# An encoder trunk on one core: every engine in program order, with wider feed-forward products

## The chip, the cores and the metric

The kernel runs on one core of a Trainium2 chip. The core has a matrix engine (TensorE, PE in the profile), a vector engine (VectorE, DVE), a scalar engine (ScalarE, ACT), a general engine (GpSimd, POOL) and a queue that starts transfers (SyncE, SP). PE writes its products to PSUM, which has eight banks of 128 partitions by 512 fp32 numbers here; everything else lives in SBUF. Each engine works through its own queue in order, and the queues meet only at semaphores. The metric is the device time of one execution in microseconds; a lower time is better.

## The reference

Two layers (`DEPTH`) of an encoder work on 256 tokens of 1024 channels. Cut to what matters:

```python
proj = x @ w_in[i]                                   # 13,824 columns, split into ten parts
y_a = multiscale_pool(a_in) @ w_branch_a[i]
y_b = dilated_attention_mixer(q, k, v) @ w_branch_b[i]
y_c = hgrn2_bidirectional(q_h, i_h, ff_h, fb_h, g_h) @ w_branch_c[i]
merged = sigmoid(gate0) * y_a + sigmoid(gate1) * y_b + sigmoid(gate2) * y_c
x1 = layer_norm(ALPHA * x + merged @ w_out[i], ln1_g[i], ln1_b[i])
hidden = silu(x1 @ w_ffn_gate[i]) * (x1 @ w_ffn_up[i])
ple = (p[i] @ w_ple_proj[i]) * sigmoid(x1 @ w_ple_gate[i])
x = layer_norm(ALPHA * x1 + hidden @ w_ffn_down[i] + ple, ln2_g[i], ln2_b[i])
```

The recurrence (`hgrn2_bidirectional`) runs in both directions over eight heads; within blocks it is written as products of scaled queries and keys. All is fp32.

## The kernel before

**Weights.** All weights are read once, as 107 chunks a layer of 1 MB, in the order of use. A chunk is loaded by SP (`dma_chunk`, L190) into one of three `raw` buffers and split by `split_chunk` (L201): ACT writes the rounded high part `whi` (L210), DVE the rest `wlo` (L211), three buffers each. `use_chunk` hands the pair to PE. A product of two split operands is three products on PE: high by high, high by low, low by high (`mm3`, L250). The residual stream is kept split as well (`xh`, `xl`), transposed to channels by tokens.

**Forms of products.** `gemm_cols` (L256) holds 128 weight columns in the array and streams 256 tokens past them, so 48 products of 256 columns use one chunk. `tok_block` (L284) holds 128 tokens and streams 512 weight columns; it takes both chunks of a block for token tile 0 and then for tile 1, and calls its evacuation after each tile. `rows_gemm` (L806) does the two row-wise projections, `w_out` (4 chunks) and `w_ffn_down` (11 chunks), into four banks: the last 2 or 3 chunks are held back, run for tile 0, then for tile 1, and each tile's layer norm (L317) follows its sums.

**Steps and background.** After each chunk `step_end` (L245) splits a later chunk and calls `background` (L225), which gives 3,000 units to the first three tasks of a list. A task is a generator; it yields its estimated cost after each piece, or `None` to sleep until the next step. Tasks are the recurrence of two heads (`hgrn_task`, L348: on DVE scans, reciprocals and scalings for each direction; then PE products L431 within blocks, L439 and L444 across blocks; masks, products L468/L469 with the values, a root mean square by four squares on ACT and a power on POOL (L302), scalings L484, a transpose and a split), attention of one head (`attn_task`, L501: scores, softmax on DVE and ACT, transposes, products L536 to L539, for two token tiles), pooling, and a transposition of the merged branches (`turn`). One recurrence task may hold the work buffers at a time (`busy`). `finish(kind)` (L241) drains tasks at once where their results or buffers are needed; `finish("attn0")` stands at L701, after the product of chunk 4 of the second pair of heads.

**Order.** The planner of the tile framework orders each engine's queue from the dependences, the order of writing and its own cost model. Only the very start is pinned: L592 to L652 put ACT, DVE and PE in program order for the first block. Elsewhere the planner may move an instruction ahead of others on its engine, transfers included: the table `p` is loaded through ACT's queue at L796, right ahead of its transposes (L802), after which `ln1`'s gains are loaded and `rows_gemm` runs. The PSUM banks are two pools of four, `g` for chunk products and `t` for the tasks.

**Feed-forward.** For each of 11 pairs of chunks, gate and up go into one bank each; ACT takes the silu (L873), DVE the product with up (L876), and `split_to` (L290) splits the result.

## Time and profile before

| | before |
|---|---|
| median of 3 runs | 1334.33 us (1334.32 to 1334.39) |
| profiled execution, its own time | 1334.35 us |
| span from first to last instruction | 1332.6 us |
| mean granted clock of TensorE | 0.996 |
| DMA, mean over the span | 175 GB/s, 51.6% of the 16 engines on SP's queue |

How to read the profile: PE and PEld are TensorE's products and its weight loads. A number like L211 is a line of the kernel; where a helper records every operation, all have one line, and the names of the tiles tell them apart (`wlo<-raw,whi` is written from `raw` and `whi`). In the timeline the columns are start and duration in microseconds, engine, line, operation, tiles, shape, count, and in brackets the idle time ahead with what ended it. Products are pipelined, so the duration of one is longer than the distance to the next. In groups, the last numbers are busy microseconds, mean nanoseconds of one, and idle time just before.

### The profile page before, as it was taken

How to read it: one execution, taken by the hardware profiler on the slowest of the kernel's cores; microseconds unless marked ns; L12 is line 12 of the kernel's file. 1: busy time of each engine (PE TensorE's matmuls, PEld its weight loads, DVE VectorE, ACT ScalarE, POOL GpSimd, SP SyncE). 2: the span in 40 equal slices, each digit the busy share in tenths (PEclk: the TensorE clock that was granted, in tenths of full speed). 3: DMA queues.
4: the chain of work that ended last, by engine and by line, in shares of the span. 5: the costliest groups of instructions: out<-in, count | busy, mean ns of one | idle time of the engine just before them, and what ended most of it. 6: DMA issues, size and time to landing. Idle time of an engine off the chain costs nothing.

```text
span 1332.6 us, 20047 instructions
## 1 busy us (share of the span) xinstructions
PE 1308.5 (98%) x8585; PEld 1185.8 (89%) x8585; DVE 867.5 (65%) x1126; ACT 587.1 (44%) x644; POOL 16.7 (1%) x24
## 2 busy tenths in 40 slices
PE   8999999999999999999989999999999999999997
PEld 6899999998888799998779999999988887999986
DVE  4598887575656855554555999875846658554445
ACT  5444444544444443443334444445534444444431
POOL 0000000000000000000000000000000000000000
PEclk9999999999999999999989999999999999999999
DMA  8654545244556475655356555442455664755551
GB/s 310 196 185 158 166 151 159 96 158 159 197 190 228 151 233 179 189 190 190 126 176 203 169 172 166 158 159 90 134 189 190 202 217 154 226 189 190 180 194 38
DMA packets 160280, 233.43 MB, mean 175 GB/s; under 512 B 3840, under 2 KB 108864, under 8 KB 160192
## 3 DMA queue, kind: packets, MB, share of 16 engines
q1 hardware_dynamic: 158496, 227.44, 51.6%
q10 hardware_dynamic: 1696, 4.72, 1.1%
q8 instruction: 67, 1.10, 0.3%
q14 instruction: 21, 0.17, 0.0%
HBM read 231.10 MB, written 1.05 MB: 174 GB/s over the span
## 4 chain that ended last, share of the span: by engine, by line
PE 93%; DVE 4%; ACT 1%; issue 1%; POOL 1%; DMA 0%; POOLq 0%; DVEq 0%; ACTq 0%
PE g L252 28%; PE g L253 28%; PE g L254 28%; DVE wlo L211 2%; PE t L444 1%; PE t L431 1%; PE t L439 1%; PE t L312 1%; POOL rs_y L302 1%; PE t L468 1%; PE t L469 1%; ACT whi L210 0%; DVE ln_st L326 0%; PE t L508 0%; PE t L528 0%
## 5 line engine op out<-in xcount | busy, mean ns | idle before, releaser
L211 DVE TENSOR_TENSOR wlo<-raw,whi 128x2048 fp32r<-128x2048 f32 (+2 forms) x218 | 489.8, 2249 | 347.4 <-ACT whi L210 347.0
L210 ACT ACTIVATE whi<-raw 128x2048 fp32r<-128x2048 f32 (+2 forms) x218 | 409.9, 1883 | 517.5 <-issue 220.7
L252 PE MATMUL g<-xh,whi 128*128 128x256 f32 x1600 | 455.6, 285 | 0.0
L254 PE MATMUL g<-xh,wlo 128*128 128x256 f32 x1600 | 453.1, 283 | 0.0
L253 PE MATMUL g<-xl,whi 128*128 128x256 f32 x1600 | 453.0, 283 | 0.0
L252 PEld LDWEIGHTS g<-xh,whi 128*128 128x128 f32 x1600 | 307.0, 192 | 0.2
L253 PEld LDWEIGHTS g<-xl,whi 128*128 128x128 f32 x1600 | 307.0, 192 | 0.2
L254 PEld LDWEIGHTS g<-xh,wlo 128*128 128x128 f32 x1600 | 306.9, 192 | 0.0
L252 PE MATMUL g<-whi,xh 128*128 128x512 f32 x480 | 190.2, 397 | 1.3 <-ACT whi L210 1.2
L253 PE MATMUL g<-wlo,xh 128*128 128x512 f32 x480 | 189.5, 395 | 1.4 <-DVE wlo L211 1.4
L254 PE MATMUL g<-whi,xl 128*128 128x512 f32 x480 | 188.1, 393 | 0.0
L253 PEld LDWEIGHTS g<-wlo,xh 128*128 128x128 f32 x480 | 91.8, 191 | 21.4 <-DVE wlo L211 3.1
L252 PEld LDWEIGHTS g<-whi,xh 128*128 128x128 f32 x480 | 91.8, 191 | 21.2 <-ACT whi L210 1.8
L254 PEld LDWEIGHTS g<-whi,xl 128*128 128x128 f32 x480 | 91.6, 191 | 19.1
L253 PE MATMUL g<-wlo,s 128*128 128x512 f32 x224 | 87.5, 391 | 0.0
L254 PE MATMUL g<-whi,s 128*128 128x512 f32 x224 | 87.5, 390 | 0.0
L252 PE MATMUL g<-whi,s 128*128 128x512 f32 x224 | 87.1, 390 | 0.0
L252 PE MATMUL g<-whi,sa 128*128 128x512 f32 x160 | 62.8, 393 | 0.0
L253 PE MATMUL g<-wlo,sa 128*128 128x512 f32 x160 | 62.5, 390 | 0.0
L254 PE MATMUL g<-whi,sb 128*128 128x512 f32 x160 | 62.3, 389 | 0.0
L253 PEld LDWEIGHTS g<-wlo,s 128*128 128x128 f32 x224 | 42.1, 188 | 9.0 <-DVE wlo L211 0.4
L254 PEld LDWEIGHTS g<-whi,s 128*128 128x128 f32 x224 | 42.0, 188 | 8.6
(168 smaller groups left out, 1136.2 us busy)
## 6 DMA issues: line engine op xcount, KB each, us to landing
raw<-in_w_in_dram SPq DMA_DIRECT2D x106, 1024.0 KB, 5.1
raw<-in_w_ffn_gate_dram SPq DMA_DIRECT2D x22, 1024.0 KB, 5.3
raw<-in_w_ffn_up_dram SPq DMA_DIRECT2D x22, 1024.0 KB, 5.3
raw<-in_w_ffn_down_dram SPq DMA_DIRECT2D x22, 1024.0 KB, 4.9
raw<-in_w_branch_c_dram SPq DMA_DIRECT2D x8, 1024.0 KB, 5.1
raw<-in_w_branch_a_dram SPq DMA_DIRECT2D x8, 1024.0 KB, 5.0
raw<-in_w_out_dram SPq DMA_DIRECT2D x8, 1024.0 KB, 4.9
raw<-in_w_ple_gate_dram SPq DMA_DIRECT2D x8, 1024.0 KB, 5.1
```

What stands on the lines that cost most here:

```text
L210: A.activation(out=hi[:, ks, :], in_=t[:, ks, :], func=AF.Copy)
L211: V.tensor_tensor(out=lo[:, ks, :], in0=t[:, ks, :], in1=f(hi[:, ks, :]), op=ALU.subtract)
L252: PE.matmul(ps, lhsT=ah, rhs=bh, start=first, stop=False)
L253: PE.matmul(ps, lhsT=ah, rhs=bl, start=False, stop=False)
L254: PE.matmul(ps, lhsT=al, rhs=bh, start=False, stop=last)
L302: G.tensor_tensor(out=y, in0=v, in1=mhalf.to_broadcast([P, n]) if n > 1 else mhalf, op=ALU.pow)
L312: PE.transpose(ps[:, k * P:(k + 1) * P], xt[:, t, (4 * hf + k) * P:(4 * hf + k + 1) * P], ident)
L431: PE.matmul(dg[po:po + 64, co:co + 64], lhsT=KI[:, cs], rhs=QI[:, cs], start=True, stop=True)
L439: PE.matmul(cr[po:po + 64, co:co + 64], lhsT=KL[:, h, 4 * t, :], rhs=QL[:, h, 4 * t, :], start=True, stop=True)
L444: PE.matmul(lg[:, co:co + P], lhsT=kp.rearrange("p b u -> p (b u)"), rhs=qp.rearrange("p b u -> p (b u)"), start=True, stop=True)
L468: PE.matmul(o, lhsT=at[:, 2 * h + t, :], rhs=vt[:, t, hs], start=True, stop=False)
L469: PE.matmul(o, lhsT=al[:, 2 * h + 1 - t, :], rhs=vt[:, 1 - t, hs], start=False, stop=True)
```

## The change

Four engines (ACT, DVE, PE and POOL) issue in program order for the whole kernel; SP is left to the planner. The order is written anew. `step_end` runs background work first, then an evacuation that is handed to it, then the split. `tok_block` uses chunk by chunk for both token tiles. The norms become a class whose sums are added early; between stages, `Handover` puts tile 0's norm under tile 1's last products, and tile 1's norm under the first products of the next stage; two chunks' splits go in quarters there, their low parts on POOL.

Three products change. The feed-forward products take the high weights against 512 columns, the high and low parts of the tokens side by side in `xx`, and the low weights against 256; the halves are added afterwards. In the recurrence, direction 0 keeps its scaled blocks, and both directions' cross-block products run together after direction 1, those that write the two halves of the partitions in turn. And the order of the three products of a token block may be by pass, so that the low parts come last.

```diff
+    ctx.enter_context(tc.manual_schedule(engines={
+        mybir.EngineType.Activation, mybir.EngineType.DVE, mybir.EngineType.PE, mybir.EngineType.Pool}))
...
-    def split_chunk():
+    def split_begin():
...
+        def piece(ks, engine=V):
+            A.activation(out=hi[:, ks, :], in_=t[:, ks, :], func=AF.Copy)
+            engine.tensor_tensor(out=lo[:, ks, :], in0=t[:, ks, :], in1=f(hi[:, ks, :]), op=ALU.subtract)
+            if ks.stop == k:
+                dma_chunk()
+        return k, piece
...
-    def step_end():
+    def step_end(then=None):
+        background()
+        if then is not None:
+            then()
         split_chunk()
-        background()
...
+    def gemm_wide(w, ps):
+        for m in range(2):
+            ms = slice(m * P, (m + 1) * P)
+            for k in range(KD):
+                wide = (ps[m], w[0][:, k, ms], xx[:, k].rearrange("p a t -> p (a t)"))
+                narrow = (ps[m][:, 0:S], w[1][:, k, ms], xx[:, k, 0, :])
+                for i, (o, a, b) in enumerate((wide, narrow) if k == 0 else (narrow, wide)):
+                    PE.matmul(o, lhsT=a, rhs=b, start=k == 0 and i == 0, stop=k == KD - 1 and i == 1,
+                              skip_group_check=True)
+
+    def joined(ps, dst):
+        for m in range(2):
+            A.activation(out=dst[:, m, :], in_=ps[m][:, 0:S], func=AF.Copy)
+            V.tensor_tensor(out=dst[:, m, :], in0=dst[:, m, :], in1=ps[m][:, S:2 * S], op=ALU.add)
...
+    def tok_block(act, evac, n=2):
+        ps = [gbank(), gbank()]
+        for i in range(n):
+            w = use_chunk()
+            for t in range(2):
+                tok_part(ps[t], w, i, n, act, t)
+            step_end((lambda: [evac(t, ps[t]) for t in range(2)]) if i == n - 1 else None)
...
+        def rest(self, then=None):
...
+            G.tensor_tensor(out=y, in0=ve, in1=mhalf, op=ALU.pow)
+            cs = [slice(512 * hf, 512 * hf + 512) for hf in range(2)]
+            for c in cs:
+                V.scalar_tensor_tensor(out=xt[:, t, c], in0=xt[:, t, c], scalar=mv[:, 0:1], in1=gb[:, 0, c],
+                                       op0=ALU.subtract, op1=ALU.mult)
+            r = small([P, 1], "ln_r")
+            newton(r, y, ve, 1)
...
             u = 31 if fwd else 0
-            tot = c4(Ct)[:, :, :, :, u:u + 1]
+            tot = small([P, 2, 4, 2, 1], "tot")
+            V.tensor_copy(out=tot, in_=c4(Ct)[:, :, :, :, u:u + 1])
...
+            across.append((QL, KL))
             if d == 0:
-                cr, lg = tbank(), tbank()
+                continue
+            cr, lg = tbank(), tbank()
             for h in range(2):
                 for t in range(2):
-                    po = 0 if fwd else 64
                     co = (2 * h + t) * 64
-                    PE.matmul(cr[po:po + 64, co:co + 64], lhsT=KL[:, h, 4 * t, :], rhs=QL[:, h, 4 * t, :],
-                              start=True, stop=True)
...
+                    for po, (Q, K) in zip((0, 64), across):
+                        PE.matmul(cr[po:po + 64, co:co + 64], lhsT=K[:, h, 4 * t, :], rhs=Q[:, h, 4 * t, :],
+                                  start=True, stop=True)
+            for h in range(2):
+                for e, (Q, K) in enumerate(across):
...
+                    PE.matmul(lg[:, co:co + P], lhsT=kp.rearrange("p b u -> p (b u)"),
+                              rhs=qp.rearrange("p b u -> p (b u)"), start=True, stop=True)
...
         rsqrt(r, ms, 4)
         yield 700
+        yield None
...
+                step_end(ev_f)
                 if d == 1:
                     tasks.append(("hgrn", hgrn_task(l, hp, q, *fk, vt, gt, oh, ol)))
-                step_end()
...
+            a, b = (n - 2, use_chunk()), (n - 1, use_chunk())
+            for hf in range(2):
+                part(*a, 0, hf)
+                part(*b, 0, hf)
+                norms[0].add(hf, banks[0][hf])
+            return banks, part, a, b
...
+            def __init__(self, norms, banks, part, a, b):
+                self.norm = norms[1]
+                norms[0].rest()
+                part(*a, 1, 0)
+                part(*b, 1, 0)
+                norms[1].add(0, banks[1][0])
+                part(*a, 1, 1)
+                k, piece = split_begin()
+                ks = [slice(j * k // 4, (j + 1) * k // 4) for j in range(4)]
+                for j in ks[:2]:
+                    piece(j, G)
+                part(*b, 1, 1, (0,))
+                ps = turn_x(0, 0)
+                split_x(0, 0, ps)
+                part(*b, 1, 1, (1,))
+                ps = turn_x(0, 1)
+                split_x(0, 1, ps)
+                for j in ks[2:]:
+                    piece(j, G)
+                norms[1].add(1, banks[1][1])
+                k, piece = split_begin()
+                ks = [slice(j * k // 4, (j + 1) * k // 4) for j in range(4)]
+                piece(ks[0], G)
+                norms[1].rest()
+                for j in ks[1:]:
+                    piece(j, G)
...
         for c in range(NF // 2):
-            pg, pu = gbank(), gbank()
-            gemm_cols(use_chunk(), xk, pg)
...
+            pg, pu = [gbank(), gbank()], [tbank(), tbank()]
+            gemm_wide(use_chunk(), pg)
+            s, u = misc([P, 2, S]), misc([P, 2, S])
+            def ev_g():
+                joined(pg, s)
+                A.activation(out=s, in_=s, func=AF.Silu)
+            def ev_u():
+                joined(pu, u)
+                V.tensor_tensor(out=s, in0=s, in1=u, op=ALU.mult)
+                i = 2 * (c % 2)
+                split_to(hs[c // 2][:, 0, i:i + 2, :], hs[c // 2][:, 1, i:i + 2, :], s)
+            step_end(ev_g)
+            gemm_wide(use_chunk(), pu)
+            step_end(ev_u)
```

After a `Handover` the next stage begins with token tile 0, pass by pass; `norm1.finish()` then transposes and splits tile 1: behind the `w_ple_proj` products and one half block after the first norm, and 32 products into the next layer after the second. The lines of `finish("attn0")` and of the load of `p` and its transposes are as they were.

## The prediction

> **What bounds the kernel now.** I read the page first, then the table of windows, then the timeline of TensorE (PE) inside the windows that lose time.

> ```profile
> PE 1308.5 (98%) x8585; PEld 1185.8 (89%) x8585; DVE 867.5 (65%) x1126; ACT 587.1 (44%) x644; POOL 16.7 (1%) x24
> ```

> PE is the bound: 98% busy. So a microsecond is won only if PE issues fewer or shorter products, or loses one of its few stops; work moved on VectorE (DVE) or ScalarE (ACT) costs nothing until PE waits for it. A busy PE need not be at its best pace, so I take the pace from starts of neighbouring products.

> ```profile
> 39.78 0.39 PE L253 MATMUL g<-wlo,xh 128*128 128x512 f32 x1
> 41.82 0.39 PE L253 MATMUL g<-wlo,xh 128*128 128x512 f32 x1
> 559.83 0.28 PE L252 MATMUL g<-xh,whi 128*128 128x256 f32 x1
> 561.99 0.28 PE L252 MATMUL g<-xh,whi 128*128 128x256 f32 x1
> ```

> Nine products of 512 columns lie between the first two rows: 2.04/9 = 0.227 us each. Eighteen of 256 columns lie between the last two: 2.16/18 = 0.120 us each. Twice 0.120 is 0.240, so each product pays about 0.0133 us beside its columns.

> ```profile
> 230.00:300.00 70.00, 69.38 (x549) 66.36 (x548) 47.39 (x106) 34.25 (x62) 1.01 (x1) 1.00 0.37 121
> 432.00:470.00 38.00, 36.08 (x165) 29.13 (x164) 30.32 (x42) 16.81 (x17) 1.84 (x2) 1.00 0.48 155
> 470.00:602.00 132.00, 132.00 (x1081) 131.08 (x1080) 68.26 (x48) 57.02 (x47) 0.00 (x0) 1.00 0.61 195
> 660.00:690.00 30.00, 25.14 (x102) 19.98 (x101) 19.50 (x23) 13.13 (x12) 0.92 (x1) 0.89 0.40 137
> ```

> Each row has the window, its length and PE's busy time first. The feed-forward stage (470 to 602) has no idle PE. The stops sit at the norms (432 to 470, 660 to 690, where the granted clock falls to 0.89), and a little in the attention stage (0.62 us).

> **Gains, step by step.**

> *Feed-forward products.* A chunk has 2x8 places with three 256-column products each, 3x0.120 = 0.360 us; `gemm_wide` issues one of 512 and one of 256, 0.347 us. 16x0.0133 = 0.213 us a chunk, 44 chunks: **-9.4 us**.

> *Cross-block products of the recurrence.* One direction of one task in the old order:

> ```profile
> 113.23 0.40 PE L254 MATMUL g<-whi,xl 128*128 128x512 f32 x1
> 113.56 0.69 PE L431 MATMUL t<-w 128*64 128x64 f32 x16
> 114.08 0.40 PE L439 MATMUL t<-w 128*64 128x64 f32 x4
> 114.41 0.49 PE L444 MATMUL t<-w 128*128 128x128 f32 x2
> 114.83 0.45 PE L439 MATMUL t<-w 128*64 128x64 f32 x4
> 115.20 0.49 PE L444 MATMUL t<-w 128*128 128x128 f32 x2
> 115.65 0.28 PE L253 MATMUL g<-xl,whi 128*128 128x256 f32 x1
> ```

> The chunk product at 113.23 ends its slot at 113.46; at 115.65 the stream is one 0.120 slot further: 2.07 us, twice a task, 4.14. L431 writes the two halves of the partitions in turn and runs two products side by side: 16 records in 0.52 us. L439 writes one half only: 4 records in about 0.24 us, and each change between 64 and 128 columns costs about 0.2 us (114.41 to 114.83 holds 0.42 for a pair that takes 0.224 elsewhere). New, direction 0 has only L431 with a change on each side, 0.09+0.52+0.20 = 0.8 us. Direction 1 has 0.09+0.52, eight paired products at L431's pace 0.47, one change 0.20 and four wide products of 0.224, 0.90: 2.2 us. 4.14-3.0 = 1.1 us, eight tasks: **-8.8 us** (nothing paired: -5).

> *Norms.*

> ```profile
> 457.45 1.29 PE L312 MATMUL t<-ident,x 128*128 128x128 f32 x8 [1.25 <-DVE x L337]
> 659.00 0.66 PE L312 MATMUL t<-ident,x 128*128 128x128 f32 x4 [0.56 <-DVE x L337]
> 674.42 1.97 PE L312 MATMUL t<-ident,x 128*128 128x128 f32 x8 [3.47 <-DVE x L337]
> 677.24 0.63 PE L252 MATMUL g<-whi,xh 128*128 128x512 f32 x1
> 677.66 0.63 PE L253 MATMUL g<-wlo,xh 128*128 128x512 f32 x1
> ...
> 1324.01 0.69 DVE L323 TENSOR_TENSOR x<-x,g 128x512 f32<-128x512 f32 x1 [1.17 <-PE g L254]
> 1328.26 1.42 DVE L337 SCALAR_TENSOR_TENSOR x<-x,ln_r,s 128x512 f32<-128x512 f32 x2
> ```

> Between the layers PE stops 0.56 us and then 30-25.14 = 4.9 us in the window from 660 (3.47 of it at 674.42), 5.4 in all, and after the last stop a 512-column product takes 0.43 us instead of 0.227: half clock, 0.11x30 = 3.3 us of that window. Together 8.7. In the new order 21 products (4.8 us) stand between the end of token tile 0's sums and its first transpose, while the norm's chain needs about 4.9: in the undisturbed last norm 4.25 from the second sum (1324.01) to the scaling (1328.26), less 0.4 as the root now runs behind both subtractions, plus 0.2 before and 0.8 until PE may turn. A stop of 0.1. Tile 1's transposes come 32 products (7.3 us) later, its last weight pieces run on GpSimd (POOL). A POOL subtraction of 128x512 is not in the trace.

> ```profile
> masks.py:199 POOL TENSOR_SCALAR_AFFINE_SELECT ident<-ident 128x128 f32<-128x128 f32 x1 | 0.3, 292 | 0.0
> ```

> That is POOL's widest elementwise row. I take four times it, 1.2 us; from below stands DVE's 0.69 for the same shape (502.56 further down), from above 2.4, twice the row for two inputs instead of one. At 1.2 the inverse root queues behind one piece for about 1.5 us and three stops of 0.2 to 0.3 remain: 0.8 in all, and no half clock: **-7.9 us**. At 2.4 a piece the three pieces ahead of the root bring 3.6 more here and about 1 at each norm 1; at 0.69 nothing remains.

> Norm 1: 149 products of 0.227 and 16 transposes of 0.11 (one record each, half of the two-record 0.224 below) are 35.6 of the window's 38 us, so 2.4 us are lost, stops and slow restarts together; now 5.4 us of `w_ple_proj` products cover it too, 0.1 is left: **-4.6 us** for two. The last norm gains the same **0.4** at the end of the kernel.

> Sum of gains: 9.4+8.8+7.9+4.6+0.4 = 31.1 us.

> **What the strict order costs.** Before, the planner pulled chunk products between dependent steps; now nothing fills them.

> *The attention flush.* I counted the tasks' costs through the 3000-unit budgets. At chunk 4 of the second pair of heads, `finish("attn0")` finds the last recurrence task before its masks, head A before its first turning and head B before its softmax. Seven rounds follow with no chunk product between.

> ```profile
> L514 DVE CUSTOM_DVE_ANT_0 m<-t,kc 128x512 f32<-128x512 f32 x16 | 10.9, 688 | 3.8 <-PE t L510 3.8
> L519 ACT ACTIVATE m<-m,nm 128x512 f32<-128x512 f32 x16 | 11.6, 725 | 19.9 <-DVE nm L517 19.6
> L530 ACT ACTIVATE m<-t 128x512 f32<-128x512 f32 x16 | 9.1, 594 | 5.0 <-PE t L528 5.0
> L474 ACT ACTIVATE m<-t 128x128 f32<-128x128 f32 x32 | 8.4, 289 | 0.0
> L484 DVE SCALAR_TENSOR_TENSOR s<-t,rms,s 128x128 f32<-128x128 f32 x32 | 9.0, 344 | 0.2
> L302 POOL TENSOR_TENSOR rs_y<-ms,mhalf 128x4 f32<-128x4 f32 x8 | 8.1, 1012 | 493.2 <-DVE t L417 255.1 <-DVE ms L476 238.1
> 127.04 0.39 PE L468 MATMUL t<-s,m 128*128 128x128 f32 x2
> 128.61 0.39 PE L469 MATMUL t<-s,m 128*128 128x128 f32 x2
> ```

> From the end of that chunk: PE works to 4.4 (a small product is 1.57/7 = 0.224). ACT's copy for B ends at 5.1, the four squares at 6.1, POOL's root at 7.4, four small DVE steps at 8.1. Only then come A's second softmax (0.69+0.73 and small steps, 2.7 us, 10.8), four DVE scalings (0.34 each, overlapping, 11.9; they free A's bank), A's turning, B's softmax (14.6), B's turning, copy and last products: 16.6. PE's own work in this is 9.4 us, so 7.2 us stand still, for about 0.6 in the old window: **+13.2 us** for two layers. Below: 0, if PE's work were filled as before.

> *The load of p.* L796 issues it on ACT's queue, and the transposes of it are the next thing on PE.

> ```profile
> L796 ACTq DMA_DIRECT2D s<-in_p_dram x2: 385/409/433, 378.1 to 1039.9; - x2
> DMA to landing us min/median/max: 3.2/3.9/4.6
> 420.51 1.92 ACT L210 ACTIVATE whi<-raw 128x2048 fp32r<-128x2048 f32 x1 [0.76 <-PE g L254]
> 420.51 0.34 ACTq L343 DMA_DIRECT2D s<-in_ln_g_dram  x1
> ```

> Before it went out at 378.1, over 40 us ahead of its transposes. In program order it stands behind the split that waits for the last branch chunk. The last two rows show that a DMA goes out as the split ahead of it starts, so PE waits one landing, 3.9 us (3.2 to 4.6), and `w_out` waits behind it: **+7.8 us**.

> *Half clock after these stops.* The 3.47 us stop brought half clock, the 1.25 us one did not; 3.9 is nearer the first. I charge both p stops 2.7 us, under the 3.3 seen, as part of the slow time falls into the stop: **+5.4 us** (0 to 13 if the flush's stops of 3 us count too). [...]

> *The feed-forward evacuation.* The two halves of each product must now be added. In program order a loop closes over two engines: split on DVE, two additions, ACT's silu (or DVE's product and ACT's copy), split on ACT, split on DVE.

> ```profile
> 498.40 1.92 ACT L210 ACTIVATE whi<-raw 128x2048 fp32r<-128x2048 f32 x1 [3.36 <-issue]
> 500.35 2.29 DVE L211 TENSOR_TENSOR wlo<-raw,whi 128x2048 fp32r<-128x2048 f32 x1 [0.77 <-ACT whi L210]
> 502.56 0.69 DVE L294 TENSOR_TENSOR sa<-m,sa 128x512 fp32r<-128x512 f32 x1
> L294 DVE TENSOR_TENSOR s<-t,s 128x256 fp32r<-128x256 f32 x8 | 3.2, 418 | 0.0
> ```

> Starts: 1.95 from split to split, 2.21 to the next DVE operation, 0.34 and 0.45 for two 256-column additions, 0.5 for the silu: 5.45 us. The up step adds the 0.7 product: 6.15. A pair needs 11.6 us; PE's pair is 32x0.347 = 11.1. The lag grows 0.5 us a pair from about 6.9 to the 11.3 that two chunks in hand allow, reached after nine of eleven pairs: **+1.6 us** for two layers.

> In the recurrence stage the same tasks now take six steps instead of seven, since direction 0 no longer sleeps after its products. By an estimate from the groups' rows DVE then has about 37 us (layer 0) or 40 (layer 1) of work for PE's 39 in six steps; weights are split two chunks ahead, and these 5 us in hand hide it. Cost 0; without that cover about 2 us. Also at 0, under PE's products: the 16 small copies of the decay totals, the evacuations ahead of the splits, and the token blocks chunk by chunk, whose evacuation comes half a block later but into four banks. The start stays as it was: its transposes and splits were in program order already.

> Sum of costs: 13.2+7.8+5.4+1.6 = 28.0. 1334.35 (span 1332.6) -31.1+28.0 = **1331.2 us**; the median of the runs, 1334.33, is the same.

> **Rivals.**
> - *The load of p is early after all* (the order binds ACT's computing but not its DMAs): 7.8 and 5.4 go, 1318. For it: both layers' loads were early before. Against it: the order is set for the whole engine.
> - *The gaps are small*, because the flush finds less left than I counted and the load is early; only the 1.6 stays: 1305. The old window's 0.62 us speaks for it, the emitted order against it.
> - *The feed-forward loop binds* (slower). If additions and hand-overs take their full durations, a pair is 2x(1.92+2.29)+4x0.42+0.69+2x0.60 = 12.0, and hand-overs of 0.05 make 12.4: 11x1.3-4.4 = 10 us a layer, 18 over my term: 1349. It decides from about 11.8 us a pair. DVE's 68 busy us of 132 speak against it.
> - *The change does less on PE than it says* (pairing fails): 1335.

> **How the numbers follow.** Forecast 0.5 (own range 1322 to 1341), p early 0.15, small gaps 0.1, feed-forward loop 0.15, less pairing 0.1. Within 0.2% (about what a measurement here can tell from none) is 1331.7 to 1337. Of the forecast's half, 0.27 lies below, 0.13 inside, 0.1 above. Faster 0.27+0.15+0.1 = 0.52; same 0.13+0.07 = 0.2; slower 0.28. The range 1313 to 1345 cuts the small gaps and the worst of the loop.

> **What would show it.** Right: 512 and 256 alternating at 0.347 us a pair; L444's successors in one run of eight records; no stop over 0.5 us between the layers; a stop of about 3.9 us before p's transposes; several stops of 1 to 3 us around the attention flush. Wrong: a p load issued long before, chunk products inside the flush, or PE idle in the feed-forward stage.

## The result and the profile after

The changed kernel takes 1384.5 us (median of 4 runs, 1381.8 to 1387.6) against 1334.36 us: a ratio of 1.038, interval 1.035 to 1.040. It is slower by 50 us, where 3 us less were forecast; the range ended at 1345. The profiled execution took 1385.6 us, its span is 1383.8.

The page of the changed kernel: its span, the busy time of its engines (share, instructions), the granted clock in 40 slices, and the shares of the chain of waits that ended last.

```profile
span 1383.8 us, 18885 instructions
PE 1317.2 (95%) x7881; PEld 1160.1 (84%) x7881; DVE 910.9 (66%) x1224; ACT 615.1 (44%) x750; POOL 49.5 (4%) x48
PEclk9999999999899999999999999998988999999999
PE 74%; DVE 11%; ACT 8%; issue 5%; POOL 1%; DMA 1%; ACTq 0%; DVEq 0%; SPq 0%; POOLq 0%
```

PE issues 704 products fewer and yet is busy 8.7 us longer: part of its work runs at half clock (mean granted clock 0.970, 0.996 before). 66.6 us of the span are without PE work (24.1 before). The chain of waits, 93% PE before, now runs through DVE and ACT for 19%. So the loss is stops and their half clock, and they can be found by stage. From the timeline of PE I took the start of each stage's first weight product; each stage reaches to the start of the next, the very last one to the start of its last weight product; both layers added (us):

| stage | before | changed | planner (run e7) | strict only at norms (run e9) |
|---|---|---|---|---|
| token blocks | 100.6 | 98.8 | 94.8 | 93.2 |
| recurrence stage | 226.4 | 225.0 | 225.0 | 225.0 |
| attention and pooling inputs | 246.4 | 255.9 | 239.6 | 239.6 |
| first branch | 93.1 | 92.7 | 92.7 | 92.7 |
| pooling mix | 13.6 | 42.3 | 13.3 | 13.3 |
| second and third branch | 152.7 | 165.7 | 153.1 | 153.2 |
| `w_out` | 45.6 | 52.0 | 45.6 | 47.8 |
| `w_ple_proj`, `w_ple_gate` | 63.6 | 66.3 | 67.2 | 56.4 |
| feed-forward | 253.4 | 246.1 | 246.1 | 246.1 |
| `w_ffn_down` | 121.4 | 122.3 | 123.0 | 120.4 |

The feed-forward stage wins 7.3 us, as it was to. The pooling mix, of which the prediction does not speak, loses 28.7. Here it is in layer 0: three timelines, PE first, then ACT, then DVE.

```profile
341.84 0.28 PE L271 MATMUL t<-h,wlo 128*128 128x256 f32 x1
349.24 0.58 PE L269 MATMUL t<-h,whi 128*128 128x256 f32 x1 [7.12 <-DVE s L335]
...
353.25 0.58 PE L269 MATMUL t<-h,whi 128*128 128x256 f32 x1 [1.08 <-DVE s L335]
```

```profile
340.63 0.63 ACT L331 ACTIVATE h<-h 128x512 fp32r<-128x512 f32 x1 [4.79 <-DVE h L644]
341.17 3.70 ACT L216 ACTIVATE whi<-raw 128x2048 fp32r<-128x2048 f32 x2
344.77 0.45 ACT L334 ACTIVATE s<-t,vec 128x256 fp32r<-128x256 f32 x1
```

```profile
343.10 2.29 DVE L217 TENSOR_TENSOR wlo<-raw,whi 128x2048 fp32r<-128x2048 f32 x1 [1.11 <-ACT whi L216]
345.30 1.28 DVE L845 SCALAR_TENSOR_TENSOR s<-s,g 128x512 f32<-128x512 f32 x2
346.50 2.29 DVE L217 TENSOR_TENSOR wlo<-raw,whi 128x2048 fp32r<-128x2048 f32 x1
348.70 0.48 DVE L335 SCALAR_TENSOR_TENSOR s<-t,vec,s 128x256 fp32r<-128x256 f32 x1
```

The mix writes the two halves of a bank (m = 0, 1), and the program says: products of half 0, take half 0 out, products of half 1, take half 1 out. PE's half 1 waits until half 0 has been read (L334 on ACT, L335 on DVE), and these stand in their queues behind two weight splits and, on DVE, two evacuations of the branch before. The planner had put the products of both halves of a bank in one run, ahead of the read. In the kernel before, the last product of half 0 and the first of half 1 of the first bank are 0.11 us apart:

```profile
338.08 0.28 PE L254 MATMUL t<-h,wlo 128*128 128x256 f32 x1
338.19 0.28 PE L252 MATMUL t<-h,whi 128*128 128x256 f32 x1
```

Whether half 1, which goes to other columns of the bank, has to wait for that read at all (7.12 us here), no run shows: that the halves could overlap was not tried.

The two hand-overs show a second cost that was not foreseen. Between the layers, token tile 1's norm on DVE, GpSimd beside it, and PE's transposes that wait:

```profile
692.06 3.00 DVE L392 SCALAR_TENSOR_TENSOR x<-x,ln_mv,s 128x512 f32<-128x512 f32 x2
695.50 1.23 DVE L340 TENSOR_TENSOR rs_t<-rs_y 128x1 f32<-128x1 f32 x1 [0.44 <-POOL rs_y L389]
696.77 1.19 DVE L341 TENSOR_TENSOR rs_t<-rs_t,ln_ve 128x1 f32<-128x1 f32 x1
697.99 0.15 DVE L342 TENSOR_SCALAR rs_t<-rs_t 128x1 f32<-128x1 f32 x1
698.17 1.00 DVE L343 TENSOR_TENSOR ln_r<-rs_t,rs_y 128x1 f32<-128x1 f32 x1
```

```profile
687.34 7.18 POOL L217 TENSOR_TENSOR wlo<-raw,whi 128x512 fp32r<-128x512 f32 x5 [1.85 <-ACT whi L216]
694.47 0.99 POOL L389 TENSOR_TENSOR rs_y<-ln_ve,mhalf 128x1 f32<-128x1 f32 x1
695.44 3.72 POOL L217 TENSOR_TENSOR wlo<-raw,whi 128x512 fp32r<-128x512 f32 x3
```

```profile
700.11 1.94 PE L353 MATMUL t<-ident,x 128*128 128x128 f32 x8 [3.80 <-DVE x L397]
```

The root (L389) queues behind five pieces, and DVE's one-number steps take 1.0 to 1.2 us beside GpSimd's pieces instead of 0.15 to 0.16; the step with one tensor input (L342) is untouched.

Last, the load of `p`: its one line (durations, starts), its landing, and the transposes that wait for it; then ACT's queue at its first start.

```profile
L902 ACTq DMA_DIRECT2D s<-in_p_dram x2: 385/406/428, 439.2 to 1126.3; - x2
DMA to landing us min/median/max: 4.4/4.5/4.5
L908 PE MATMUL t<-ident,s 128*128 128x128 f32 x8 | 2.2, 435 | 8.7 <-DMA s<-in_p_dram 8.7
```

```profile
439.16 1.91 ACT L216 ACTIVATE whi<-raw 128x2048 fp32r<-128x2048 f32 x1 [3.52 <-PE g L316]
439.17 0.43 ACTq L902 DMA_DIRECT2D s<-in_p_dram  x1
```

It goes out as the split ahead of it on ACT's queue starts, and PE stands still for 8.7 us in two layers: as forecast.

### The profile page after: what moved, and what is told of

It reads as the page before. It is cut to its first block, busy times and chain, and to the rows that moved or that the text cites. A ratio compares the mean times of both kernels' runs of the same rounds, so it can differ in the third digit from the quotient of the medians.

```text
span 1383.8 us, 18885 instructions
## 1 busy us (share of the span) xinstructions
PE 1317.2 (95%) x7881; PEld 1160.1 (84%) x7881; DVE 910.9 (66%) x1224; ACT 615.1 (44%) x750; POOL 49.5 (4%) x48
## 4 chain that ended last, share of the span: by engine, by line
PE 74%; DVE 11%; ACT 8%; issue 5%; POOL 1%; DMA 1%; ACTq 0%; DVEq 0%; SPq 0%; POOLq 0%
PE g L316 31%; PE g L269 11%; PE g L270 11%; PE g L271 11%; ACT whi L216 7%; DVE wlo L217 5%; DVE m L296 2%; DVE m L1028 1%; PE g L289 1%; POOL wlo L217 1%; PE t L494 1%; PE t L596 1%; DMA s<-in_p_dram 1%; PE t L353 1%; PE t L511 1%
## 5 line engine op out<-in xcount | busy, mean ns | idle before, releaser
L316 PE MATMUL g<-whi,xx 128*128 128x512 f32 x960 | 300.4, 399 | 1.2 <-ACT whi L216 1.2
L269 PE MATMUL g<-xx,whi 128*128 128x256 f32 x896 | 256.2, 286 | 0.0
L271 PE MATMUL g<-xx,wlo 128*128 128x256 f32 x896 | 253.4, 283 | 0.0
L270 PE MATMUL g<-xx,whi 128*128 128x256 f32 x896 | 253.4, 283 | 0.0
L316 PEld LDWEIGHTS g<-whi,xx 128*128 128x128 f32 x960 | 184.2, 193 | 39.7 <-ACT whi L216 1.6
L316 PE MATMUL g<-wlo,xx 128*128 128x512 f32 x480 | 186.2, 396 | 0.0
L269 PEld LDWEIGHTS g<-xx,whi 128*128 128x128 f32 x896 | 171.7, 192 | 0.6
L270 PEld LDWEIGHTS g<-xx,whi 128*128 128x128 f32 x896 | 171.9, 192 | 0.2
L271 PEld LDWEIGHTS g<-xx,wlo 128*128 128x128 f32 x896 | 171.7, 192 | 0.0
L289 PE MATMUL t<-xx,whi 128*128 128x512 f32 x352 | 123.6, 396 | 0.0
L289 PE MATMUL g<-xx,whi 128*128 128x512 f32 x352 | 123.6, 396 | 0.0
L316 PEld LDWEIGHTS g<-wlo,xx 128*128 128x128 f32 x480 | 92.7, 193 | 20.0 <-DVE wlo L217 0.3
L289 PE MATMUL g<-xx,wlo 128*128 128x256 f32 x352 | 90.9, 279 | 0.0
L289 PEld LDWEIGHTS g<-xx,whi 128*128 128x128 f32 x352 | 64.5, 188 | 12.0
L289 PEld LDWEIGHTS t<-xx,whi 128*128 128x128 f32 x352 | 64.5, 188 | 11.9
L289 PEld LDWEIGHTS t<-xx,wlo 128*128 128x128 f32 x352 | 66.3, 188 | 3.9
L289 PEld LDWEIGHTS g<-xx,wlo 128*128 128x128 f32 x352 | 66.3, 188 | 3.9
```

The costliest lines, as they stand in the source:

```text
L269: PE.matmul(ps, lhsT=ah, rhs=bh, start=first, stop=False)
L270: PE.matmul(ps, lhsT=ah, rhs=bl, start=False, stop=False)
L271: PE.matmul(ps, lhsT=al, rhs=bh, start=False, stop=last)
L289: PE.matmul(o, lhsT=a, rhs=b, start=k == 0 and i == 0, stop=k == KD - 1 and i == 1, skip_group_check=True)
L316: PE.matmul(ps, lhsT=a, rhs=b, start=i == 0 and k == 0 and p == 0, stop=i == n - 1 and k == 3 and p == 2)
```

## The experiments

Each edit is to the changed kernel unless it says otherwise. The differences below are taken between ratios to the kernel before, times 1334 us.

**e1: the mix's products first.**

```diff
                         (mh[:, k, :], ml[:, k, :]), k == 0, k == 1)
+            for m in range(2):
                 i = 2 * g + m
                 split_to(ph[:, i, :], pl_[:, i, :], ps[:, m * S:(m + 1) * S], vec[:, 8 * l + i:8 * l + i + 1])
```

> The changed kernel, but in the pooling mix each group's products for both halves of a bank are issued before the two halves are taken out of it. Theory: in strict order PE's second half of a bank waits until the first half is read out by ACT and DVE, which stand behind two weight splits (stops of 7.12 and three times 1.08 us at 342 to 361, and half clock from 347.6 to 360.8); with the products first, four banks take all of them without a wait. The stage falls from 20.8 and 21.5 us to 6.8 each and the stop is gone: 1384.5 - 28 = about 1356 us. Rival: PE waits there for the pooling tasks themselves, which are drained just before; then only the three short stops go with their half clock, and the time stays above 1372.

1352.3 us, ratio 1.014 (1.012 to 1.015): 32 us less. The stage takes 5.7 us in each layer, and its products follow each other every 0.12 us. Rows from this stretch of PE's timeline in e1:

```profile
343.15 0.28 PE L269 MATMUL t<-h,whi 128*128 128x256 f32 x1
343.26 0.28 PE L270 MATMUL t<-h,whi 128*128 128x256 f32 x1
...
347.43 0.28 PE L269 MATMUL t<-h,whi 128*128 128x256 f32 x1
347.55 0.28 PE L270 MATMUL t<-h,whi 128*128 128x256 f32 x1
```

The theory holds; the pooling tasks drained just before were not what PE waited for.

**e2: `p` loaded after the first half of the last branch.**

```diff
             if n == 0:
                 tasks.append(("turn", turn_later(0)))
+                pT = slot("s7", [P, 2, S])
+                nc.scalar.dma_start(out=pT, in_=p[l, 0].rearrange("(t p) c -> p t c", p=P))
...
-        pT = slot("s7", [P, 2, S])
-        nc.scalar.dma_start(out=pT, in_=p[l, 0].rearrange("(t p) c -> p t c", p=P))
```

> The changed kernel, with the load of p issued on the same queue after the first half of the last branch instead of right ahead of its transposes. Theory: the stop of 4.78 us (layer 0) and 4.69 us (layer 1) ahead of those transposes is the landing of this load, and the half clock for 6.8 us after it (3.4 us lost) is its consequence: 2 x (4.5 + 3.4) = 16 us less, about 1368.5 us, full clock at 440 to 460. Rival: the stop would be there anyway, since the split or the transposed branch that w_out needs is as late; then less than 4 us are won and the stop moves to the next product.

1372.4 us, 1.028 (1.025 to 1.030): 13 us less. The stop is gone in both layers: the last branch falls from 49.7 to 44.8 us in each, and `w_out`, which had run at half clock behind it (0.50 from 442.8 to 449.6 us in layer 0), by 2.4 and 1.9. That is 14 us of the 16 expected, by stages. The time agrees to 1 us, with runs that spread over 7.

**e3: the pieces on DVE.**

```diff
                 for j in ks[:2]:
-                    piece(j, G)
+                    piece(j)
...
-                piece(ks[0], G)
+                piece(ks[0])
```

> The changed kernel, with the weight pieces of both hand-overs subtracted on DVE instead of GpSimd, in the same places. Theory: GpSimd's pieces (1.39 us each) cost the norm of token tile 1 twice, by the root that queues behind them (2.3 us) and by DVE's steps that take 1.2 us instead of 0.15 beside them (4.6 us); on DVE the five pieces ahead of the scaling cost 3.5 us in the same chain and the small steps are back at 0.15 to 0.2. The stops of 3.3 and 4.2 us shrink to about 2 each; 3 to 8 us less in all, 1377 to 1381. Rival: DVE is the scarcer engine there and the pieces on it only add to the chain: the stops grow by 1 us or more and the time rises to 1388 or over.

1372.6 us, 1.029 (1.028 to 1.031): 11 us less, more than either theory said. The same norm, on DVE alone:

```profile
691.11 0.68 DVE L217 TENSOR_TENSOR wlo<-raw,whi 128x512 fp32r<-128x512 f32 x1
691.71 0.20 DVE L385 BATCH_NORM_AGGREGATE ln_mv<-ln_st 128x2 f32<-128x12 f32 x1
691.94 0.16 DVE L387 TENSOR_SCALAR ln_ve<-ln_mv 128x1 f32<-128x1 f32 x1
692.01 1.41 DVE L392 SCALAR_TENSOR_TENSOR x<-x,ln_mv,s 128x512 f32<-128x512 f32 x2
693.34 0.15 DVE L340 TENSOR_TENSOR rs_t<-rs_y 128x1 f32<-128x1 f32 x1
693.52 0.16 DVE L341 TENSOR_TENSOR rs_t<-rs_t,ln_ve 128x1 f32<-128x1 f32 x1
```

L392 is back from 3.00 to 1.41 us for its pair and L340 from 1.23 to 0.15. Five pieces cost DVE 3 us ahead of the scaling, but on GpSimd they had cost the chain 5: from the start of L392 to that of L340 3.44 instead of 1.33, and 2.9 in the three small steps. The stops ahead of tile 1's transposes got shorter by 2.7 to 2.8 us each (3.80 to 1.13 between the layers, 2.92 to 0.13 after `w_out`), and part of the half clock went with them, which I had not counted: between the layers it lasted from 698.7 to 705.6 us in the changed kernel, while in e3 the four products from 696.04 took 1.83 us and the next four, from 697.71, were back at 1.09, the full pace.

**e4: the norm ahead of the second split, that split on DVE.**

```diff
+                norms[1].rest()
                 k, piece = split_begin()
                 ks = [slice(j * k // 4, (j + 1) * k // 4) for j in range(4)]
-                piece(ks[0], G)
-                norms[1].rest()
-                for j in ks[1:]:
-                    piece(j, G)
+                for j in ks:
+                    piece(j)
```

> The changed kernel, with the norm of token tile 1 ahead of the whole second weight split of a hand-over, and that split on DVE; the first split stays on GpSimd. Theory: the root then starts at once, GpSimd is idle beside the scaling, and the transposes of tile 1 find their input ready: the stops of 3.3 us (two norms after w_out) and 4.2 us (between the layers) fall under 0.6 us, and with them the half clock of 1.7 and 3.4 us behind: 2 x 5 + 7.6 = 17 us less, about 1367. Rival: the second split is then late itself and PE waits for its low part instead; then under 8 us are won.

1369.4 us, 1.027 (1.025 to 1.028): 14 us less. Between the layers the transposes of tile 1 find their input ready:

```profile
690.85 1.98 PE L316 MATMUL g<-whi,xx 128*128 128x512 f32 x8
692.67 1.04 PE L353 MATMUL t<-ident,x 128*128 128x128 f32 x8
```

The stages of `w_ple_gate` fall by 5.0 us each, the token blocks of layer 1 by 5.6. The theory holds; PE does not wait for the second split.

**e5: the flush's rounds spread over chunks 2 to 4.** `gemm_cols` calls `between` ahead of its second, third and fourth quarter.

```diff
-                gemm_cols(use_chunk(), xk, ps)
+                gemm_cols(use_chunk(), xk, ps,
+                          between=(lambda: background(10 ** 9)) if jp == 1 and 2 <= i <= 4 else None)
```

> The changed kernel, with the rounds of the tasks that finish of attn0 drains at once issued between the quarters of the chunk products 2, 3 and 4 of the second pair of heads. Theory: the stops of 1.0 to 2.8 us at 245 to 259 and 930 to 945 (6.5 us of idle PE in a layer, and 3.4 to 5 us lost to the half clock behind) come from dependent steps with no chunk product between; with products between, both go: 2 x (6.5 + 3.4 to 5) = 20 to 23 us less, about 1363; no stop over 1 us is left there. Rival: DVE is the bound of that stretch, so its steps ahead of the weight splits make the chunk products wait instead; then under 10 us are won, 1375 or more.

1393.6 us, 1.045 (1.043 to 1.046): 9 us **more**. The theory failed. The rival named the right engine, DVE, but not the right wait: every stop of PE in this stretch stands ahead of a task's own product, none ahead of a chunk product. PE in e5, and DVE's split ahead of the third of these stops:

```profile
225.40 0.69 PE L496 MATMUL t<-w 128*64 128x64 f32 x16 [1.38 <-DVE w L454]
228.96 2.05 PE L513 MATMUL t<-w 128*128 128x128 f32 x8 [1.68 <-DVE sb L337]
248.63 1.22 PE L578 MATMUL t<-h 128*128 128x256 f32 x2 [5.66 <-DVE mx L584]
```

```profile
243.71 2.29 DVE L217 TENSOR_TENSOR wlo<-raw,whi 128x2048 fp32r<-128x2048 f32 x1 [6.00 <-ACT whi L216]
```

A round without a limit on its budget takes each task to its next sleep, so the third recurrence task's long DVE steps came ahead, and its products (L496) stood in PE's queue before their input was there. Later DVE had its softmax (L584) behind a weight split whose high part came 6 us late: a stop of 5.66 us. Products between the rounds did not help here, since steps that were not ready stood ahead of them.

**e6: e1, e2, e4 and e5 together.**

> All four edits together: products first in the pooling mix, p loaded early, the second split after the norm and on DVE, the rounds spread. Theory: the four places are independent, so the gains add: 32 (measured) + 12 to 16 + 15 (measured) + 20 = 79 to 83 us below 1384.5, that is 1302 to 1306, below the kernel before by 2.2%; mean granted clock at 0.995 or more. Rival: the stops shift into one another; then the sum falls short by 10 us or more, 1313 and over.

1332.5 us, 0.999 (0.998 to 1.000). The gains and e5's loss add: 32+13+14-9 = 50 us, 51 were measured. What is missing to 1304 is e5's failure: the two attention stages take 131.7 us in layer 0, 127.8 in the changed kernel, 119.8 under the planner.

**e7: the planner again.** The new writing and the products stay.

```diff
-    ctx.enter_context(tc.manual_schedule(engines={
-        mybir.EngineType.Activation, mybir.EngineType.DVE, mybir.EngineType.PE, mybir.EngineType.Pool}))
```

> The changed kernel without its first statement: the planner orders all engines again, the writing and the three product changes stay. Theory: what was lost is lost to the strict order, so with the planner the stops in the pooling mix, at p and in the attention flush are filled as before, the products keep their 16 us, and the norms gain at most some: 1334 - 16 to - 24 = 1310 to 1318. Rival: the new writing itself (evacuations behind background work, hand-overs, GpSimd pieces) is what costs; then the time stays at 1330 or over.

1323.0 us, 0.993 (0.991 to 0.995). Pooling mix, `w_out` and the branches are as before (table), the attention stages gain 6.8 us against before. The theory holds for the strict order: it costs 60 us against the same program planned. It was 5 us too hopeful: the first block begins 4.8 us later, since its pin went as well, and the norm after `w_out` loses 1.8 us a layer.

**e8: e6 with the old feed-forward products.** One bank a product, no addition of halves; up is treated as gate is here.

```diff
-            pg, pu = [gbank(), gbank()], [tbank(), tbank()]
-            gemm_wide(use_chunk(), pg)
+            pg, pu = gbank(), gbank()
+            gemm_cols(use_chunk(), xk, pg)
...
-                joined(pg, s)
-                A.activation(out=s, in_=s, func=AF.Silu)
+                A.activation(out=s, in_=pg.rearrange("p (m t) -> p m t", t=S), func=AF.Silu)
```

> The four edits of the run before, and the feed-forward products as before the change: three of 256 columns at each place, one bank a product, no addition of halves. Theory: the wide products won 16 x 0.0133 us in each of 44 chunks less a small residue, 7.3 us by the two stages: this kernel is 7 to 9 us slower than the four edits alone. Rival: the additions on ACT and DVE cost more elsewhere (splits later, stage after stage) and the wide products are worth under 4 us.

1338.5 us, 1.003 (1.002 to 1.005): 6 us slower than e6, short of the 7 to 9. The feed-forward stages take 7.3 us more, but `w_ffn_down` behind them 1.7 less. With the wide products PE stops there for a weight split (its group in the changed kernel: 0.9 us in two layers; none in e8); the other 0.8 us is not traced to a row:

```profile
L270 PE MATMUL g<-wlo,sb 128*128 128x512 f32 x32 | 12.7, 396 | 0.9 <-DVE wlo L217 0.9
```

**e9: strict order only around the norms.** The planner orders all but three stretches: the first block, `w_out` to the first `w_ple_gate` block, the layer boundary; with e4's edit.

```diff
+    def order_on():
+        st = ExitStack()
+        st.enter_context(tc.manual_schedule(engines={
+            mybir.EngineType.Activation, mybir.EngineType.DVE, mybir.EngineType.PE, mybir.EngineType.Pool}))
+        strict.append(st)
+    def order_off():
+        strict.pop().close()
...
+        order_on()
         norms = [Norm(t, gb, ALPHA) for t in range(2)]
...
+        order_off()
         tok_block(xtok, lambda t, ps: ev(1, t, ps))
```

> The planner orders everything but three stretches in strict order: the first block, w_out with the norm after it up to the second product of w_ple_gate, and the last layer boundary with its norm; the second split of a hand-over late and on DVE; the other three edits left out, since the planner does them. Theory: strict order pays where the order is written around a norm and costs where products must be pulled between tasks. Against the run with the planner alone (1323): the start wins 4.8 us back, the stages w_out to w_ple_gate 56.4 to 52.1 us twice, the boundary another 3.4: 1323 - 17 = about 1306. Rival: the stops only move to the borders of the stretches, where neither order reaches across; then it stays at 1316 or over.

**1306.1 us** (1305.9 to 1306.3), 0.980 (0.978 to 0.981), as forecast: the fastest version, 27 us below the kernel before. Its three terms came as well: 4.4, 8.5 and 4.3 us by stage against e7, for 4.8, 8.6 and 3.4. Since e4's edit is in it, the run does not show what strict order alone is worth there; the planner with e4's edit was not tried. Its windows (busy time of PE, PEld, DVE, ACT, POOL, then granted clock, DMA share, GB/s) over a part of the attention stages that holds all their idle time, the pooling mix, the norm after `w_out` and the boundary:

```profile
240.00:260.00 20.00, 19.28 (x158) 18.39 (x156) 10.74 (x28) 10.99 (x26) 1.01 (x1) 1.00 0.25 83
330.00:350.00 20.00, 20.00 (x113) 17.33 (x112) 13.62 (x14) 9.70 (x13) 0.00 (x0) 1.00 0.53 181
430.00:470.00 40.00, 39.90 (x186) 32.98 (x185) 33.13 (x47) 19.84 (x25) 7.39 (x6) 1.00 0.58 189
640.00:670.00 30.00, 29.79 (x137) 23.90 (x136) 22.40 (x38) 12.65 (x17) 7.33 (x6) 1.00 0.44 141
```

Around the attention and the two norms, the windows of the kernel before had lost 0.6, 1.9 and 4.9 us of PE; here it is 0.7, 0.1 and 0.2, at full clock.

**e10: as e6, with the rounds only in the quarters of chunks 4 and 5, chunk 4 taken out after both.**

```diff
+                late = jp == 1 and i >= 4
+                gemm_cols(use_chunk(), xk, ps, between=(lambda: background(10 ** 9)) if late else None)
+                if late and i == 4:
+                    background(10 ** 9)
+                    split_chunk()
+                    ps4 = ps
+                    continue
+                if late:
+                    finish("attn0")
...
```

> As the run with all four edits, but the rounds are spread only over chunks 4 and 5 of the second pair, in quarters, and chunk 4 is taken out after both. Theory: the earlier spreading failed because it pulled the third recurrence task's long DVE steps ahead, so that its products stood in PE's queue before their input was there (stops of 1.4 and 1.7 us) and a weight split then stood ahead of a softmax (5.7 us); left where they were, the seven rounds find 11 us of products between them. The two attention stages of a layer together fall from 131.7 to 124 us or less, and the time from 1332.5 to 1316 or less. Rival: in strict order any chunk's split ahead of a dependent step holds it, wherever the rounds are; then the stages stay at 128 or over and the time at 1325 or over.

1314.4 us, 0.986 (0.984 to 0.987). The attention stages take 122.3 and 123.6 us. The theory holds: strict order can be written much better here too, though this writing does not reach the planner's 119.8.

## Why the prediction was wrong, point by point

**The step that failed is "What the strict order costs".** It rested on one sentence, "before, the planner pulled chunk products between dependent steps; now nothing fills them", and looked for dependent steps only where the diff or a task list had them: the attention flush, the load of `p`, the feed-forward loop. The pooling mix stands in no line of the diff. Its loop always had the order product, read, product in one bank, and only the planner had hidden it. That is 28.7 us of the 53 that the forecast missed (e1: 32 with what follows).

**"Three stops of 0.2 to 0.3 remain: 0.8 in all, and no half clock"** was the second failure. Tile 0's part was right: its first transposes followed the 21 products after stops of 0.1 us between the layers and 0.3 after `w_out`. GpSimd's piece was sized well (1.39 us for 1.2, within 0.69 to 2.4). But I let the root queue behind one piece for 1.5 us, and it stood behind five and waited 2.3 us after its input (L387) was there; and that DVE's small steps would take up to 1.23 us instead of 0.15 beside GpSimd's pieces was nowhere in the sum. The boundary won 1.6 us instead of 7.9 (`w_ffn_down` of layer 0 61.6 to 61.8, token blocks of layer 1 52.8 to 51.1), and the norms after `w_out` lost 2.7 in the two stages behind them and 2.2 more in `w_out`, where tile 0's transposes now stand (47.8 in the runs without the stop for `p`, 45.6 before), instead of winning 4.6: about 16 us in all. e3 and e4 each take both causes away at once; the rows above tell them apart. With e4's edit the gains are there: in e10 7.2 us at the boundary and 5.0 at the two norms after `w_out`, close to the 7.9 and 4.6 of the sum.

**The half clock after the flush** was set to 0, with the true case only in brackets ("if the flush's stops of 3 us count too"). They count. The windows of about 3.4 us ahead of two changes to half clock, and one ahead of none:

```profile
248.10:251.60 3.50, 1.14 (x6) 0.90 (x6) 1.94 (x9) 0.82 (x2) 0.41 (x1) 1.00 0.00 0
480.30:483.70 3.40, 1.53 (x10) 1.30 (x11) 2.58 (x4) 0.83 (x2) 0.89 (x1) 1.00 0.33 80
244.70:248.10 3.40, 1.95 (x16) 1.52 (x14) 0.17 (x1) 1.63 (x9) 0.60 (x1) 1.00 0.02 6
```

After the first row the clock was 0.50 until 258.4, after the second until 487.1; after the third it stayed at 1.00. So 1.1 or 1.5 us of PE work in such a window did not keep the clock up. The flush as a whole, stops and clock, cost 16 us (attention stages 255.9 us, 239.6 under the planner) for 13.2 in the sum; its stops alone are 12.3. By stage, the profiled executions miss the forecast by 54 us: 32 at the mix with the branch behind it, 16 at the norms, 3 at the flush, and 3 in small parts.

**Right in kind and nearly in size:** the load of `p`, 8.7 us for 7.8, and the half clock for 6.8 us after each stop: with e2 the branch and `w_out` together fall by 3.0 and 2.5 us more than the stops themselves, for 2.7 each. The recurrence's products: 0.82 and 2.2 us a task for 0.8 and 2.2, 9 us won. The new unit of direction 1:

```profile
112.44 0.69 PE L494 MATMUL t<-w 128*64 128x64 f32 x16
112.96 0.64 PE L504 MATMUL t<-w 128*64 128x64 f32 x16
113.53 1.16 PE L511 MATMUL t<-w 128*128 128x128 f32 x8
```

The pairing of L504 is seen in 16 records of 0.57 us. A feed-forward pair takes 0.350 us in the mean (0.347): 7.3 us won in its stages for 9.4 in the sum, without a stop. The cost of its evacuation, 1.6, came as 1.7, but a stage later (e8); so the net is 6 for 7.8. The kernel's end won nothing: it is 0.7 us longer instead of 0.4 shorter, which I did not follow up.

**The rivals.** None held the result. The one on the slower side put its price on the feed-forward loop, and that loop never bound. The rival with an early load of `p` fell; the load stood in ACT's order, as forecast.

## What to carry to other kernels

Before an order is fixed by hand, walk each engine's queue through the whole program, untouched loops included, and ask of every product into a bank that has been partly read what its reader stands behind (here L335 behind two weight splits, a stop of 7.12 us). Fix the order only where it was written with care: here strict order everywhere gave 1384 us as first written and 1314 after four mends (e10), and strict order only in the first block and around the norms, with one of these mends, 1306. And work given to an idle engine was not free here: beside GpSimd's pieces the dependent chain on DVE got longer (L340 took 1.23 us instead of 0.15), and its root, on GpSimd itself, came 2.3 us late.

## What the hardware showed

**GpSimd and DVE.** Beside GpSimd's subtraction some of DVE's steps with two tensor inputs took longer: L340 1.23 us instead of 0.15 for one number, L392 3.00 instead of 1.41 for a pair of 128x512. L342, with one input, kept 0.15, and L377, whose second input is the bank `g`, its 0.68. The steps of one number, 1.0 to 1.2 us, came near the length of one piece (1.39 us); why, no run shows.

```profile
351.00:354.40 3.40, 2.32 (x11) 2.02 (x11) 0.97 (x2) 0.88 (x2) 0.00 (x0) 0.50 0.68 262
354.40:357.80 3.40, 2.32 (x11) 2.02 (x10) 0.97 (x2) 0.95 (x2) 0.00 (x0) 0.50 0.00 0
```

The changed kernel's runs spread over 5.8 us and those of e9 over 0.5; whether it matters for this where a stop falls on the grid was not tried.
